# The chunk products of a bidirectional recurrence: the two heads of a pair, one after the other or in turns

## The chip, the cores and the metric

The kernel runs on one core of a Trainium2 chip. The metric is the device time of one execution in microseconds (us), taken as the median of several runs; lower is better.

## The reference, cut to what matters

One layer of a diffusion backbone: normalise and modulate the tokens, one input projection, then two mixers side by side (a bidirectional RWKV-7 recurrence with 8 heads of 64, and 4 heads of latent attention), an output projection, and a top-4-of-32 mixture of experts over 1024 tokens. The change touches the recurrence alone. Its definition, per direction `d`, head `h` and time step:

```python
def wkv_update(S, w_t, k_t, v_t, kk_t, a_t):
    """S: (2, B, H, N_v, N_k).  S <- S diag(w) + S (-kk)^T (kk*a) + v^T k."""
    sa = jnp.einsum("dbhvk,dbhk->dbhv", S, kk_t)
    return S * w_t[..., None, :] - sa[..., :, None] * (kk_t * a_t)[..., None, :] + v_t[..., :, None] * k_t[..., None, :]

def wkv_outputs(S0, r, ops):
    def step(S, inp):
        r_t, rest = inp
        S = wkv_update(S, *rest)
        return S, jnp.einsum("dbhvk,dbhk->dbhv", S, r_t)
    S, out = lax.scan(step, S0, (r, ops))
    return S, from_time_major(out)
```

First 256 context tokens are scanned for the state alone, then 1024 latent tokens for outputs.

## The kernel before, in words

**Chunks.** The recurrence is done in chunks of 64 tokens: 20 steps `j` of `Rwkv.scan` (line 2320), 4 of the context and 16 of the latent tokens, both directions at once. The 8 heads are 4 pairs (`q` or `hp`, 0 to 3); the two heads `h` of a pair lie on partitions 0 to 63 and 64 to 127 (`HS[0]`, `HS[1]`). Per step the operands of all pairs and both directions lie in a tile `W[:, d, q, 0:256]`: columns 0 to 63 for the outputs, 64 to 127 for the state, 128 to 255 the two keys.

**Products.** `Rwkv.products` (line 2143) makes, for each step, the matrix of in-chunk products `LM` that the scan multiplies by. For each pair, direction and head it is one fp32 matmul that contracts over the 64 partitions of the head, with 128 stationary columns (`x[:, 128:256]`) and 128 moving ones (`x[:, lo:128]`; 64 in a context step, where `lo` is 64). It goes over two halves `i` of the pairs and over `h`: four matmuls into one PSUM bank, then one VectorE multiply of the bank by the causal mask into `LM` (a "group"). A step has four groups, the kernel 80: 16 with 64 moving columns and 64 with 128. An fp32 matmul shows in the profile as two MATMUL records and two LDWEIGHTS records, so a group is 8 MATMUL records of the form 64\*128 64x128 (or 64x64). After the groups the same stream scales the keys on GpSimd (POOL), transposes them on TensorE into `BT`, and `states` (line 2171) copies columns; when all are done `ready[j]` is fired, which the scan waits for.

**What sets the order.** The whole stage is written as streams (Python generators) that are woven at build time by `Weave.run` (line 1033 on). A stream yields the name of an engine ("pe", "dve", "act", "pool", "sp") and then issues instructions there; `yield "pe", slots` asks for a turn of TensorE and a free bank out of `slots` at the same moment. The planner keeps a modelled time of every engine and of every buffer, takes the engine that can start soonest, and gives the turn to the ready stream of the smallest rank. The ranks: 0 for the scan and for the solver of the triangular systems, 30 for the work beside them, 49 to 81 for attention, 60 and 61 for readout and output mixing, 70 for the preparation of chunks with `products`, 100 for the chunk outputs. When its model of the TensorE clock is about to fall, attention (`dense`) goes first. The order of each engine's instructions is then fixed; at run time each engine goes through its own queue in that order and waits on semaphores. The modelled price of a product comes from `Timed.product` (line 915): the larger of the two column counts divided by 0.6 (0.3 at the lower clock), so 213 ns (427 ns) each, whatever stands beside it. The price isn't touched by the change. Every instruction woven in this way has line 954, that of the recording helper.

**Banks.** PSUM has eight banks. The scan has two of its own and the chunk outputs two more; the other four (`front.P`, here `self.B`) are shared by the products, the transposes, the solver, attention, readout and output mixing.

**Sets.** The operands of a step live in one of three sets (`self.SET`), so chunks are prepared at most three steps ahead of the scan.

After the mixers come output mixing, routing and the experts (`Experts`, lines 382 to 423 hold its matmuls and evictions), which run from about 1285 us to the end.

Of the kernel before, what the change touches and what calls it, by code (L numbers as in the profile page):

```python
# [30 lines left out]
HS = [slice(0, 64), slice(64, 128)]  # L31
# [148 lines left out]
class Experts:  # L180
# [190 lines left out]
    def products(self, J, s):  # L371
        nc, N = self.nc, J["N"]
        p = self.rings["pe"][0]
        self.rings["pe"].reverse()
        J["p", s] = p
        if s < 8:
            X = J["X"]
            xt = X.rearrange("p k s n -> p (k s n)").bitcast(BF).rearrange("p (k s n t) -> p k s n t", k=KT, s=2, t=2)
            wh, wl = (x.rearrange("p (k s c) -> p k s c", k=KT, s=2) for x in J.pop(("c", s)))
            for q in range(2):  # L380
                for k in range(KT):
                    nc.tensor.matmul(p[:, q, :2 * N], wh[:, k, q], X[:, k].rearrange("p s n -> p (s n)"),  # L382
                                     start=k == 0, stop=False, skip_group_check=True)
            for q in range(2):
                for k in range(KT):
                    nc.tensor.matmul(p[:, q, N:2 * N], wl[:, k, q], xt[:, k, 0, :, 1],  # L386
                                     start=False, stop=k == KT - 1, skip_group_check=True)
            return
        w = J.pop(("w", s)).rearrange("p (k s c) -> p k s c", k=KT, s=2)
        late = 1 if s == 8 else 0  # L390
        order = [(q, k) for q in range(2) for k in range(KT - late)] + [(q, k) for q in range(2) for k in range(KT - late, KT)]
        for q, k in order:
            nc.tensor.matmul(p[:, q, :N], w[:, k, q], J["H"][:, k], start=k == 0, stop=k == KT - 1, skip_group_check=True)  # L393
# [1656 lines left out]
class Rwkv:  # L2050
# [92 lines left out]
    def products(self, S, lo):  # L2143
        w, K, W, LM, j = self.w, self.K, S["W"], S["LM"], S["j"]
        msk = K("mask").rearrange("p (d o x) -> p d o x", o=1, d=2)[:, :, :, lo:].to_broadcast([128, 2, 2, 128 - lo])
        yield S["loaded"]
        left = [3]
        for i in range(2):
            for h in range(2):
                p = yield "pe", self.B  # L2150
                pv = p.rearrange("p (d q x) -> p d q x", d=2, q=2)
                for d in range(2):
                    for q in range(2):
                        x = W[HS[h], d, 2 * i + q]
                        w.pe.matmul(pv[:, d, q, lo:], x[:, 128:256], x[:, lo:128], start=True, stop=True)
                yield "dve"
                w.dve.tensor_mul(LM[:, :, 2 * i:2 * i + 2, h, lo:], pv[:, :, :, lo:], msk)
                w.put(self.B, p)
        w.spawn(70, self.states(S, left))
        for d in range(2):  # L2160
            yield "pool"
            w.pool.tensor_mul(W[:, d, :, 128:256], W[:, d, :, 128:256], S["lam"][:, d, :, None].to_broadcast([128, HP, 128]))
            p = yield "pe", self.B
            for hp in range(HP):
                w.pe.transpose(p[:, hp * 128:hp * 128 + 128], W[:, d, hp, 128:256], K("ident"))
            yield "act"
            w.act.activation(S["BT"][:, d].rearrange("p q x -> p (q x)"), p, AF.Copy)
            w.put(self.B, p)
            self.count(S, left)
# [742 lines left out]
```

## Time and profile before

| what | value |
|---|---|
| median of 3 runs | 2736.94 us (2735.51 to 2742.81) |
| the profiled execution | 2734.6 us, of which its span (first to last instruction) 2732.8 us |
| TensorE matmul busy (PE) | 2548.0 us, 93% |
| TensorE weight loads busy (PEld, beside PE) | 2240.4 us, 82% |
| VectorE (DVE) | 1889.3 us, 69% |
| ScalarE (ACT) | 1461.1 us, 53% |
| GpSimd (POOL) | 508.0 us, 19% |
| mean granted TensorE clock | 0.947 of full speed |

Busy times of different engines overlap. A matmul's record lasts until its result is written, so records of consecutive matmuls overlap too: what one more matmul costs is the distance between starts, not the record's length. The chain of waits is followed back from the last instruction: at each step to what released it, or else to the instruction before it on its engine.

### The profile page before, as it was taken

How to read it: one execution, taken by the hardware profiler on the slowest of the kernel's cores; microseconds unless marked ns; L12 is line 12 of the kernel's file. 1: busy time of each engine (PE TensorE's matmuls, PEld its weight loads, DVE VectorE, ACT ScalarE, POOL GpSimd, SP SyncE). 2: the span in 40 equal slices, each digit the busy share in tenths (PEclk: the TensorE clock that was granted, in tenths of full speed). 3: DMA queues.
4: the chain of work that ended last, by engine and by line, in shares of the span. 5: the costliest groups of instructions: out<-in, count | busy, mean ns of one | idle time of the engine just before them, and what ended most of it. 6: DMA issues, size and time to landing. Idle time of an engine off the chain costs nothing.

```text
span 2732.8 us, 58537 instructions
## 1 busy us (share of the span) xinstructions
PE 2548.0 (93%) x23428; PEld 2240.4 (82%) x23428; DVE 1889.3 (69%) x3925; ACT 1461.1 (53%) x2489; POOL 508.0 (19%) x455
## 2 busy tenths in 40 slices
PE   6999886989999997986999999999999999999996
PEld 3667664678677786665999999999999999999995
DVE  7745888867776638677676675766667676766765
ACT  6323333546544533234665665766656666666664
POOL 1112564411111136210011100110101010011101
PEclk8999987879999988997999999999999999999998
DMA  6741324253243145665887896988888988889884
GB/s 259 260 150 56 110 91 161 101 150 94 87 122 106 52 145 157 234 205 203 296 326 261 312 334 252 321 323 301 324 317 309 334 295 324 308 321 323 306 334 147
DMA packets 212183, 622.50 MB, mean 228 GB/s; under 512 B 49400, under 2 KB 127352, under 8 KB 160576
## 3 DMA queue, kind: packets, MB, share of 16 engines
q1 hardware_dynamic: 201008, 581.95, 59.1%
q0 software_dynamic: 10896, 36.74, 5.5%
q8 instruction: 186, 3.05, 0.4%
q14 instruction: 93, 0.76, 0.1%
HBM read 544.09 MB, written 74.53 MB: 226 GB/s over the span
## 4 chain that ended last, share of the span: by engine, by line
PE 72%; DVE 18%; DMA 3%; issue 3%; ACT 3%; POOL 1%; SPq 1%; DVEq 0%; ACTq 0%; POOLq 0%
PE banks L954 24%; PE banks L382 18%; PE banks L393 18%; DVE at L954 14%; PE banks L386 9%; ACT at L954 2%; DVE at L356 2%; PE banks L438 2%; PE banks L326 1%; POOL at L954 1%; DVE at L408 1%; SPq L954 1%; PE banks L292 0%; DVE at L409 0%; DMA at<-vh_d 0%
## 5 line engine op out<-in xcount | busy, mean ns | idle before, releaser
L954 PE MATMUL banks<-at,at 128*128 128x512 f32 (+10 forms) x3810 | 753.4, 355 | 54.4 <-POOL at L954 18.9
L954 PEld LDWEIGHTS banks<-at,at 128*128 128x128 f32 (+3 forms) x3290 | 451.4, 188 | 209.7 <-issue 82.3
L356 DVE TENSOR_TENSOR at<-at,at 128x2048 bf16<-128x2048 f32 x252 | 576.2, 2287 | 54.8 <-ACT at L348 53.9
L382 PE MATMUL banks<-at,at 128*128 128x256 f32 (+11 forms) x4096 | 601.8, 300 | 0.0
L382 PEld LDWEIGHTS banks<-at,at 128*128 128x128 f32 x4096 | 548.7, 190 | 1.2
L393 PE MATMUL banks<-at,at 128*128 128x128 f32 (+11 forms) x4096 | 521.5, 287 | 6.6 <-DVE at L417 6.0
L393 PEld LDWEIGHTS banks<-at,at 128*128 128x128 f32 x4096 | 505.0, 191 | 13.7 <-DVE at L417 12.9
L348 ACT ACTIVATE at<-at 128x2048 fp32r<-128x2048 f32 x252 | 481.5, 1911 | 0.0
L954 ACT ACTIVATE at<-banks 128x512 f32<-128x512 f32 (+6 forms) x475 | 239.6, 525 | 362.3 <-PE banks L954 339.5
L408 DVE TENSOR_TENSOR at<-banks,at 128x256 f32<-128x256 f32 (+11 forms) x256 | 115.6, 452 | 316.3 <-ACT at L407 304.3
L954 DVE TENSOR_TENSOR at<-at,at 128x1024 fp32r<-128x1024 f32 (+26 forms) x388 | 281.3, 736 | 57.0 <-ACT at L954 38.6
L407 ACT ACTIVATE at<-banks,at 128x128 f32<-128x128 f32 (+11 forms) x512 | 189.3, 380 | 226.1 <-PE banks L386 186.8
L386 PE MATMUL banks<-at,at 128*128 128x128 bf16 (+11 forms) x4096 | 306.0, 226 | 0.0
L954 ACT ACTIVATE at<-at 128x512 f32<-128x512 f32 (+10 forms) x259 | 175.9, 701 | 202.6 <-DVE at L954 108.3
L386 PEld LDWEIGHTS <-at 128*128 128x128 bf16 x4096 | 258.1, 96 | 17.6 <-issue 3.0
L954 PE MATMUL banks<-at 128*64 128x64 f32 (+4 forms) x4880 | 231.7, 232 | 36.8 <-DMA at<-w_d 18.6
L954 PEld LDWEIGHTS banks<-at 128*64 128x64 f32 (+3 forms) x4880 | 204.8, 143 | 68.7 <-issue 18.6
L954 POOL TENSOR_TENSOR at<-at,at 64x512 f32<-64x512 f32 (+5 forms) x130 | 185.9, 1439 | 308.0 <-DVE at L954 279.5
L423 ACT ACTIVATE at<-banks,at,modc 128x128 f32<-128x128 f32 (+11 forms) x256 | 116.9, 469 | 203.7 <-PE banks L393 203.5
L954 PE MATMUL banks<-kc,at 128*128 128x128 f32 (+4 forms) x1136 | 182.7, 291 | 44.5 <-ACT at L954 17.2
L312 POOL DMA_INDIRECT at<-h_d,at x49 | 47.5, 969 | 892.0 <-DVE at L294 364.1
L954 POOL TENSOR_TENSOR at<-at 128x512 f32<-128x512 f32 (+3 forms) x94 | 129.8, 1387 | 431.2 <-PE banks L954 132.3
(155 smaller groups left out, 2015.6 us busy)
## 6 DMA issues: line engine op xcount, KB each, us to landing
at<-in_wexp SPq DMA_DIRECT2D x384, 1024.0 KB
at<-in_mod_w SPq DMA_DIRECT2D x48, 512.0 KB
at<-w_d SPq DMA_DIRECT2D x48, 384.0 KB
w_d<-at SPq DMA_DIRECT2D x16, 1024.0 KB
at<-w_d SPq DMA_DIRECT2D x32, 512.0 KB
at<-in_w_in SPq DMA_DIRECT2D x18, 512.0 KB
x_d<-at SPq DMA_DIRECT2D x18, 512.0 KB
at<-in_x SPq DMA_DIRECT2D x16, 512.0 KB
```

The source lines that it names most:

```text
L312: nc.gpsimd.indirect_dma_start(out=xg[:R], out_offset=None, in_=self.d["h2"], in_offset=bass.IndirectOffsetOnAxis(ap=gi[:R, 0:1], axis=0))
L326: nc.tensor.transpose(p[:, k, :R], xg[:R, kk * 128:kk * 128 + 128], ident[:R, :R])
L348: self.nc.scalar.activation(wh, J["w", s], AF.Copy)
L356: self.nc.vector.tensor_sub(wl, J.pop(("w", s)), wh.bitcast(F32))
L382: nc.tensor.matmul(p[:, q, :2 * N], wh[:, k, q], X[:, k].rearrange("p s n -> p (s n)"), start=k == 0, stop=False, skip_group_check=True)
L386: nc.tensor.matmul(p[:, q, N:2 * N], wl[:, k, q], xt[:, k, 0, :, 1], start=False, stop=k == KT - 1, skip_group_check=True)
L393: nc.tensor.matmul(p[:, q, :N], w[:, k, q], J["H"][:, k], start=k == 0, stop=k == KT - 1, skip_group_check=True)
L407: nc.scalar.activation(u[:, q], p[:, q, N:2 * N], AF.Identity, bias=b)
L408: nc.vector.tensor_add(u, p[:, :, :N], u)
L423: nc.scalar.activation(J["yT"][:, c], p[:, q, :N], AF.Identity, bias=J["b2"][:, 8 + c:9 + c], scale=self.gt2[:, c:c + 1])
L438: nc.tensor.transpose(p[:R, k * 128:k * 128 + 128], J["yT"][:, 4 * j + k, b0:b0 + R], self.K("ident"))
L954: return f(*args, **kw)
```

## The change

The loop over `h` moves inside. A stream now asks for two turns of TensorE, each with a bank, and issues nothing in the first; in the second it issues the eight matmuls of a half of the pairs, with the two heads alternating, head 0 into the first bank and head 1 into the second. Then the two banks are masked one after the other, each in a VectorE turn of its own, and each is given back after its own mask. The number, shapes and operands of matmuls and masks stay as they are. Ranks, model prices and everything else in the kernel stay too; the planner weaves the whole stage anew.

```diff
         for i in range(2):
+            ps = [(yield "pe", self.B)]
+            ps.append((yield "pe", self.B))
+            views = [p.rearrange("p (d q x) -> p d q x", d=2, q=2) for p in ps]
+            for d in range(2):
+                for q in range(2):
+                    for h in range(2):
+                        x = W[HS[h], d, 2 * i + q]
+                        w.pe.matmul(views[h][:, d, q, lo:], x[:, 128:256], x[:, lo:128], start=True, stop=True)
             for h in range(2):
-                p = yield "pe", self.B
-                pv = p.rearrange("p (d q x) -> p d q x", d=2, q=2)
-                for d in range(2):
-                    for q in range(2):
-                        x = W[HS[h], d, 2 * i + q]
-                        w.pe.matmul(pv[:, d, q, lo:], x[:, 128:256], x[:, lo:128], start=True, stop=True)
                 yield "dve"
-                w.dve.tensor_mul(LM[:, :, 2 * i:2 * i + 2, h, lo:], pv[:, :, :, lo:], msk)
-                w.put(self.B, p)
+                w.dve.tensor_mul(LM[:, :, 2 * i:2 * i + 2, h, lo:], views[h][:, :, :, lo:], msk)
+                w.put(self.B, ps[h])
```

## Rows read from the trace of the kernel before

**Rows 1.** Busy time by engine in the stage of the recurrence, and in parts of it.
```profile
core 0: us, PE busy (x) PEld busy (x) DVE busy (x) ACT busy (x) POOL busy (x), PEclk, DMA share, GB/s
545.00:1130.00 585.00, 540.53 (x7020) 442.84 (x7021) 390.14 (x770) 267.43 (x494) 141.01 (x151) 0.90 0.39 118
...
950.00:1050.00 100.00, 92.05 (x1225) 81.16 (x1224) 50.04 (x92) 36.00 (x64) 38.84 (x43) 0.90 0.45 140
```

**Rows 2.** The chain of waits, 545 to 1130 us: shares; then pieces (start us, us, what).
```profile
by line: PE banks L954 54.3%; DVE at L954 28.9%; ACT at L954 4.6%; issue 4.1%; SPq L954 2.4%; DMA at<-vh_d 1.8%; POOL at L954 1.3%; DMA at<-v_d 0.7%; DMA at<-w_d 0.7%; DMA at<-in_w_out 0.6%; DMA at<-qr_d 0.4%; DMA at<-qn_d 0.4%; DVEq L954 0
...
954.88 28.98 PE banks L954 x283
```

**Rows 3.** Groups of instructions on PE, all of the span, shapes apart: the products.
```profile
L954 PE MATMUL banks<-at 64*128 64x128 f32 x512 | 75.6, 296 | 1.1 <-DVE at L954 1.1
...
L954 PE MATMUL banks<-at 64*128 64x64 f32 x128 | 19.3, 304 | 0.0
```

**Rows 4.** PE in order of time: one isolated group at full clock and what follows it.
```profile
start us, us, engine line op out<-in xcount [idle before <-releaser]
735.32 1.16 PE L954 MATMUL banks<-at 64*128 64x128 f32 x8
736.41 0.33 PE L954 MATMUL banks<-kc,at 128*128 128x128 f32 x1
```

**Rows 5.** PE in order of time, 954 to 970 us: groups at the lower clock.
```profile
954.88 1.34 PE L954 MATMUL banks<-at 64*128 64x128 f32 x8 [1.13 <-DVE at L954]
...
958.58 2.07 PE L954 MATMUL banks<-at 64*128 64x128 f32 x8
960.58 0.48 PE L954 MATMUL banks<-kc,at 128*128 128x128 f32 x1
...
963.12 2.07 PE L954 MATMUL banks<-at 64*128 64x128 f32 x8
965.12 2.50 PE L954 MATMUL banks<-at,at 128*128 128x128 f32 x10
967.55 2.07 PE L954 MATMUL banks<-at 64*128 64x128 f32 x8
```

**Rows 6.** PE in order of time: two groups that stand next to each other.
```profile
728.50 1.66 PE L954 MATMUL banks<-at 64*128 64x64 f32 x16
730.08 0.38 PE L954 MATMUL banks<-at,at 128*128 128x128 f32 x1
```

**Rows 7.** MATMUL records in flight in 10 ns: in Rows 4, in Rows 6, at lower clock.
```profile
core 0: us, PE busy (x), PEclk, DMA share, GB/s
735.90:735.91 0.01, 0.01 (x3) 1.00 0.00 0
729.33:729.34 0.01, 0.01 (x6) 1.00 0.00 0
...
964.00:964.01 0.01, 0.01 (x2) 0.50 1.11 410
```

**Rows 8.** Groups on DVE, 545 to 1130 us, shapes apart: the masks of latent steps first.
```profile
L954 DVE TENSOR_TENSOR at<-banks,kc 128x512 f32<-128x512 f32 x64 | 43.8, 689 | 34.5 <-PE banks L954 29.5 <-ACT at L954 4.2
...
L954 DVE TENSOR_TENSOR at<-banks,kc 128x256 f32<-128x256 f32 x50 | 19.4, 418 | 24.9 <-PE banks L954 14.0 <-ACT at L954 10.6
```

**Rows 9.** Who waited for whom on PE, 545 to 1130 us: us in total, times, longest.
```profile
engine line waited for: us in total, times, longest us
...
PE banks L954 <- DVE at L954: 25.9, 20, 4.8
...
PE banks L954 <- ACT at L954: 13.2, 10, 2.5
```

**Rows 10.** Groups on ACT, 545 to 1130 us: the evictions of full banks.
```profile
L954 ACT ACTIVATE at<-banks 128x512 f32<-128x512 f32 x181 | 105.3, 595 | 117.0 <-PE banks L954 112.7 <-DVE at L954 3.0
```

## The prediction

> **What bounds the kernel now.** The change sits in the stage from about 545 to 1130 us, so I read that stage and not the whole span. The busy times come first: TensorE works 540.5 of 585 us there, VectorE 390.1, ScalarE 267.4, GpSimd 141.0 [rows 1]. TensorE is 92% busy, also late in the stage when attention is over (92.05 of 100 us), and it stands still for 585 - 540.5 = 44.5 us. Its waits on VectorE and ScalarE make 25.9 and 13.2 us of that [rows 9]. The chain of waits says how much of the end hangs on it: 54.3% of the stage's chain lies on TensorE, 28.9% on VectorE, 4.6% on ScalarE [rows 2]. So a microsecond of TensorE work taken out of this stage brings about half a microsecond, and VectorE is what is late next. One piece of that chain shows the products on it: the 28.98 us from 954.88 us are TensorE alone [rows 2], and four groups of products begin inside them [rows 5].
>
> Then the products themselves. The form 64\*128 64x128 has 512 records and 64x64 has 128 [rows 3], so 80 groups of 8, or 40 pairs of groups. An isolated group at full clock, 8 records, begins at 735.32 and the next work at 736.41 [rows 4]: 1.09 us. At the lower clock (granted 0.50, the 1.2 GHz level) it takes 965.12 - 963.12 = 2.00 us [rows 5]. Counted through the whole stage in order of time, some 29 pairs consist of groups like the first, between 4 and 5 pairs run at the lower clock, and the groups of about 6 or 7 pairs stand right beside another group.
>
> Such neighbours are the evidence for this change. In rows 6 a context step's last group (head 1) is followed directly by a latent step's first group (head 0): other partitions, another bank. The 16 records take 730.08 - 728.50 = 1.58 us [rows 6] and not twice 1.09. Inside that stretch six MATMUL records are in flight at one moment, in the isolated group three [rows 7]. So the two halves of the array already work at the same time where the order happens to allow it.
>
> **The change part by part.**
>
> *Products of two heads in turns.* For two heads together the lower bound is one group's time, 1.09 us [rows 4], since every record then has a partner from the other half as in rows 7; the upper bound is 2.18 us, no gain. The neighbours at 1.58 us [rows 6] are between, because only the end of one group met the start of the next. I take 1.09 us, because six in flight against three is the full factor of two and alternating gives every matmul a partner from the start. Released on TensorE: 29 pairs at 2.18 - 1.09 = 1.09 us, 31.6 us; 4.5 pairs at the lower clock at 2.00 us, 9.0 us; 6.5 pairs that already overlap at 1.58 - 1.09 = 0.49 us, 3.2 us. Sum 44 us, between 0 and 44.
>
> *What reaches the end.* By the share of the chain, 0.543 of 44 us is 24 us [rows 2]. Not all of that lasts, since another chain closes in behind the shortened one: VectorE is 67% busy. I take a fifth off, 19 us; the ends are 0 and 44 us.
>
> *The masks move behind both heads.* Their number and size stay: a latent mask is 689 ns [rows 8]. Before, the mask of head 0 ran while TensorE went on; now two masks follow a pair, 1.38 us after 1.09 us of products. Where VectorE is the last to end (28.9% of the chain), the 0.29 us that TensorE no longer covers is paid: 40 x 0.29 x 0.289 = 3 us. It is 0 where other TensorE work stands between pairs, and 12 us if every pair pays. What is queued behind a mask on VectorE is the solver's multiplies and the scan's additions, both ahead of everything in rank, so a late mask delays them.
>
> *VectorE's wait in front of the masks.* VectorE idled 34.5 us ahead of latent masks, 29.5 us of it for TensorE [rows 8]. There is a reason in the code: the planner prices a group at 4 x 213 ns = 0.85 us, the chip takes 1.09 us, so masks were placed too early. After the change it prices eight matmuls at 1.70 us and the chip should take 1.09 us, so most of that idle time goes. Worth at most 29.5 x 0.289 = 8.5 us, at least nothing; I take half, 4 us.
>
> *Two turns and two banks.* No instruction is added. The stream takes a bank in its first turn, issues nothing, and holds the bank until a second turn with a second bank comes. By the waits on bank evictions that the stage has now (39.1 us on VectorE and ScalarE together [rows 9]) the shared four banks are not what TensorE waits for most, so I price this at nothing. What hides it is that other streams' products, transposes and scores still have two or three banks, each emptied in 595 ns [rows 10]. If that cover is gone, the second rival below has the price.
>
> *The order woven anew.* The planner's turns shift, so the whole stage gets another order. No row shows that order. Nearest are the single waits of TensorE for VectorE and ScalarE: 30 of them, 39.1 us, 1.3 us each [rows 9]. Five more or five fewer are 6 us either way; I take zero.
>
> Sum: -19 + 3 - 4 = -20 us. Against the profiled execution's own 2734.6 us that is 2714.6 us; that execution lies 2.3 us under the median of the runs, 2736.94 us, so the forecast is 2717 us.
>
> The masks are also where a rule speaks against the change. The rows show VectorE waiting in front of the masks, not TensorE waiting for them [rows 8]. The Trainium skill, TensorEngine Tiling (Array Packing), section Performance Considerations, warns that tiling speeds up TensorE but not the emptying of PSUM, which may become the bottleneck. By that rule every pair would cost its two masks' 1.38 us; 32 us would be released and not 44, 14 us of it would reach the end, the 3 us for the masks would fall away as counted already, and the forecast would be about 2719 us; by the rows it is 2717 us.
>
> **The rivals.**
>
> *All of the released time counts.* For: the 29 us piece of pure TensorE in the chain [rows 2], and a stage in which TensorE is 92% busy throughout [rows 1]. Against: 28.9% of the chain is VectorE's. It would give 2736.9 - 44 = 2693 us.
>
> *Nothing that reaches the end.* The released time turns into more standstill on TensorE, because the scan's own chain (its additions, the solver, loads and sets) sets the pace, or the heads don't overlap as hoped because the weight loads of both halves queue. For: VectorE's and the loads' share of the chain. Against: TensorE's share, and rows 6 and 7, where weights were loaded for both halves too. It gives 2733 to 2737 us.
>
> *The banks run short, slower.* Its place: between a pair's two turns, when one of the four shared banks lies empty and reserved and two more wait for their masks. If TensorE then stands still until a ScalarE eviction (595 ns [rows 10]) and a mask (689 ns [rows 8]) are over, a pair pays 1.28 us, 40 pairs 51 us, against 44 us released: some 7 to 8 us slower where all of it is on the path, 2745 us. The point from which it decides is 44 / 40 = 1.1 us of standstill per pair. For: attention, readout, solver and mixing all draw on those four banks. Against: TensorE's 39.1 us of such waits in the whole stage [rows 9].
>
> **How the numbers follow.** A measurement of this kernel can tell about 0.3% (8 us) from no change. Chances: the forecast 0.55, all of it counts 0.16, nothing reaches the end 0.17, banks run short 0.12. Faster by over 0.3% is then 0.71, within 0.3% 0.17, slower 0.12. The likeliest case alone spans 2707 to 2730 us: with 12 us instead of 3 for the masks and nothing for the wait it is 2730, with no fifth taken off and 8.5 us for the wait 2707. The range reaches down to the case in which everything counts and up to the last case's beginning: 2692 to 2744 us. Outside are the worse half of the last case and large shifts of the order, together less than 2 in 10.
>
> **What would show it.** Right: in order of time the products stand as 40 blocks of 16 records, each about 1.1 us to the next work at full clock, with about six records in flight; TensorE's busy time in the stage falls by about 40 us while the stage itself ends about 20 us earlier; VectorE's idle time before the masks shrinks. The experts after it take as long as before. Wrong: blocks of 16 that take about 2 us (no overlap); TensorE's waits on VectorE and ScalarE well above 39 us (banks); or a stage as long as before with more standstill on TensorE (hidden).

## The result, and the profile after

The changed kernel takes 2772.81 us (median of 4 runs, 2767.42 to 2781.11) against 2736.35 us of the kernel before (4 runs): ratio 1.0131, 95% interval 1.0101 to 1.0160. The forecast was 2717 us, faster. It is 36 us slower, outside the range, and on the other side.

Busy time by engine in the stage of the recurrence, kernel after; it answers to [rows 1].

```profile
core 0: us, PE busy (x) PEld busy (x) DVE busy (x) ACT busy (x) POOL busy (x), PEclk, DMA share, GB/s
545.00:1130.00 585.00, 495.11 (x6990) 401.42 (x6990) 370.94 (x741) 264.29 (x483) 136.57 (x153) 0.89 0.39 118
```

TensorE's busy time fell from 540.5 to 495.1 us, as the change meant it to. But the window is the same length, so TensorE now stands still for 90 of 585 us where it stood still for 44.5 us. The time was released and turned into waiting.

The products themselves, groups on PE with shapes apart, kernel after; they answer to [rows 3].

```profile
L954 PE MATMUL banks<-at 64*128 64x128 f32 x512 | 42.3, 300 | 2.1 <-DVE at L954 1.7 <-ACT at L954 0.5
...
L954 PE MATMUL banks<-at 64*128 64x64 f32 x128 | 12.0, 316 | 2.5 <-DVE at L954 2.4
```

75.6 + 19.3 us have become 42.3 + 12.0 us: 40.6 us less. One block in order of time, kernel after, at full clock; it answers to [rows 4].

```profile
778.71 1.16 PE L954 MATMUL banks<-at 64*128 64x128 f32 x16
779.80 0.44 PE L954 MATMUL banks<-kc,at 128*128 128x128 f32 x2
```

Both heads, 16 records, take 779.80 - 778.71 = 1.09 us, exactly what one head took before. At the lower clock it is the same: a block and the wait before it, order of time, kernel after; it answers to [rows 5].

```profile
812.76 0.82 PE L954 MATMUL banks<-kc,at 128*128 128x128 f32 x5 [2.91 <-DVE at L954]
813.51 2.08 PE L954 MATMUL banks<-at 64*128 64x128 f32 x16
815.52 0.69 PE L954 MATMUL banks<-kc,at 128*128 128x128 f32 x2
```

2.01 us for both heads, with a clock granted at 0.50. Records in flight in 10 ns, kernel after; the rows answer to [rows 7].

```profile
core 0: us, PE busy (x), PEclk, DMA share, GB/s
772.60:772.61 0.01, 0.01 (x6) 1.00 0.57 205
814.20:814.21 0.01, 0.01 (x4) 0.50 0.00 0
```

Six in flight at full clock and four at the lower one, where an isolated group had three and two. All 640 records stand in 40 blocks of 16. The alternation works. What went wrong shows in who waited for whom on PE, 545 to 1130 us, kernel after; it answers to [rows 9].

```profile
engine line waited for: us in total, times, longest us
...
PE banks L954 <- DVE at L954: 51.7, 35, 11.3
PE banks L954 <- ACT at L954: 22.8, 25, 2.5
```

TensorE waited 74.5 us for VectorE and ScalarE, before 39.1 us. (The row of 812.76 above is one of these waits, 2.91 us.) The first matmuls of the experts began at 1306.5 us, before at 1267.9 us (somewhat ahead of the 1285 us at which the experts were said to begin): the first and last starts of line 382, kernel after and then kernel before.

```profile
L382 PEld LDWEIGHTS banks<-at,at x4096: 186/188/338, 1306.5 to 2720.1; 128*128 128x128 f32 x196
```

```profile
L382 PEld LDWEIGHTS banks<-at,at x4096: 186/188/338, 1267.9 to 2681.3; 128*128 128x128 f32 x196
```

The experts take 1413.6 us from first to last in one and 1413.4 us in the other. So practically all of the 39 us between the two profiled executions arises before them. Part of it is seen in attention: in the kernel before its last score product on 64 rows starts at 946 us, in the changed kernel ten records of such products (two to a product) still run after 947 us, the last from 997 us on.

```profile
L954 PE MATMUL banks<-at,at 64*128 64x512 f32 x6 | 3.3, 545 | 0.0
...
L954 PE MATMUL banks<-at,at 64*128 64x256 f32 x4 | 1.7, 430 | 0.0
```

(Groups on PE, 947 to 1130 us, kernel after; the kernel before has none.) The masks of latent steps, groups on DVE, 545 to 1130 us, kernel after, answer to [rows 8]:

```profile
L954 DVE TENSOR_TENSOR at<-banks,kc 128x512 f32<-128x512 f32 x64 | 44.0, 688 | 25.4 <-PE banks L954 23.0
```

### The profile page after: what moved, and what is told of

The parts are those of the page before. It is cut to its first block, busy times and chain, and to the rows that moved or that the text cites. A ratio compares the mean times of both kernels' runs of the same rounds, so it can differ in the third digit from the quotient of the medians.

```text
span 2771.8 us, 58552 instructions
## 1 busy us (share of the span) xinstructions
PE 2527.6 (91%) x23428; PEld 2213.8 (80%) x23428; DVE 1896.9 (68%) x3925; ACT 1469.6 (53%) x2489; POOL 497.6 (18%) x455
## 4 chain that ended last, share of the span: by engine, by line
PE 68%; DVE 18%; issue 4%; DMA 4%; ACT 3%; POOL 1%; SPq 1%; DVEq 0%; ACTq 0%; POOLq 0%
PE banks L954 21%; PE banks L382 18%; PE banks L393 17%; DVE at L954 14%; PE banks L386 9%; ACT at L954 2%; DVE at L356 2%; PE banks L438 2%; PE banks L326 1%; POOL at L954 1%; DMA at<-w_d 1%; DVE at L408 1%; SPq L954 1%; DMA at<-y_d 1%; DMA at<-in_x 0%
## 5 line engine op out<-in xcount | busy, mean ns | idle before, releaser
L954 PE MATMUL banks<-at,at 128*128 128x512 f32 (+9 forms) x3810 | 765.3, 359 | 86.3 <-ACT at L954 40.2
L954 PEld LDWEIGHTS banks<-at,at 128*128 128x128 f32 (+3 forms) x3290 | 457.1, 191 | 245.2 <-issue 82.3
L393 PEld LDWEIGHTS banks<-at,at 128*128 128x128 f32 x4096 | 505.0, 191 | 14.0 <-DVE at L417 13.2
L954 DVE TENSOR_TENSOR at<-at,at 128x512 f32<-128x512 f32 (+26 forms) x388 | 281.9, 738 | 58.2 <-ACT at L954 39.2
L954 POOL TENSOR_TENSOR at<-at,at 64x512 f32<-64x512 f32 (+6 forms) x130 | 188.6, 1459 | 304.2 <-DVE at L954 281.2
L954 PE MATMUL banks<-at 128*64 128x64 f32 (+4 forms) x4880 | 193.4, 233 | 49.7 <-DVE at L954 31.8
L954 PEld LDWEIGHTS banks<-at 128*64 128x64 f32 (+3 forms) x4880 | 169.4, 143 | 76.6 <-DVE at L954 31.7
L954 PEld LDWEIGHTS banks<-kc,at 128*128 128x128 f32 (+2 forms) x1136 | 143.8, 172 | 88.6 <-issue 34.6
```

The costliest lines, as they stand in the source:

```text
L954: return f(*args, **kw)
```

## The experiments

Three explanations were on the table: the alternation itself costs something; the second bank, above all while it is reserved and empty, starves the other streams; the planner weaves worse, because it counts a block at 1.70 us that takes 1.09 us, or simply because a new weave is a new draw, another order of the same work that may be good or bad by chance. Ratios are to the kernel before, run on the same chip beside each experiment; it came out between 2734 and 2740 us there.

**e1, alternation undone, order kept.** The planner's price doesn't depend on the order inside a turn, so this kernel and the changed one have the same order everywhere else; in the two traces the 3925 instructions of VectorE, 2489 of ScalarE and 455 of GpSimd indeed follow in the same sequence of forms.

```diff
-            for d in range(2):
-                for q in range(2):
-                    for h in range(2):
+            for h in range(2):
+                for d in range(2):
+                    for q in range(2):
```

> The changed kernel with one thing undone: in the two-bank turn the four products of head 0 are issued first and the four of head 1 after them. The planner's prices are the same, so the order of every engine is that of the changed kernel. Theory A (alternating does what was forecast, the loss of 36 us comes from the new order and the banks): slower than the changed kernel, whose blocks take 1.09 us, by 40 blocks x (1.58 - 1.09) us = 20 us times the chain's share of TensorE there (0.37): 7 to 15 us, so 2780 to 2788 us. Rival (alternating itself costs something, because matmuls on both halves hinder neighbours or each other): as fast as or faster than the changed kernel, 2772 us or less.

Measured: 2772.12 us, ratio 1.0116 (1.0061 to 1.0172): the changed kernel's 2772.81 us. A block, order of time, kernel e1:

```profile
774.62 1.71 PE L954 MATMUL banks<-at 64*128 64x128 f32 x16
776.26 0.44 PE L954 MATMUL banks<-kc,at 128*128 128x128 f32 x2
```

Blocks take 1.64 us in place of 1.09 us, and nothing of it is seen at the end. Where it went stands in the busy times and in the waits of PE, 545 to 1130 us, kernel e1:

```profile
545.00:1130.00 585.00, 512.27 (x6975) 420.95 (x6976) 367.23 (x735) 259.16 (x474) 133.59 (x152) 0.89 0.39 116
```

```profile
PE banks L954 <- DVE at L954: 40.9, 26, 10.8
PE banks L954 <- ACT at L954: 18.4, 20, 2.5
```

TensorE is busy 17.2 us longer than in the changed kernel, and waits 59.3 us for VectorE and ScalarE where that waits 74.5 us: 15.2 us less. So in this order what the blocks save is spent waiting. Theory A's 2780 to 2788 us failed. The time is where the rival put it, but not for the rival's reason: alternating makes the blocks shorter, so it hinders nothing. With four runs on each side, a gain of up to some 7 us could not be told from none.

**e2, the two banks in one turn.** A small class stands for "two free banks", so nothing is reserved empty.

```diff
-            ps = [(yield "pe", self.B)]
-            ps.append((yield "pe", self.B))
+            ps = yield "pe", Two(self.B)
```

> The changed kernel, but the two banks are asked for in one turn, so none is reserved and empty while the second is awaited. Bank theory (the reserved empty bank starves the other streams): most of the loss returns, 2725 to 2750 us. Price theory (the planner counts 1.70 us for a block that takes 1.09 us, and weaves the rest around it): as slow as the changed kernel, 2760 to 2785 us.

Measured: 2754.98 us, ratio 1.0073 (1.0045 to 1.0101): about half of the loss returns, between the ranges of both theories.

**e3, the price that the trace shows.** In the planner's `product`:

```diff
+            elif (k, m) == (64, 128) and n in (64, 128):
+                ns = 136 if fast else 250
             else:
                 ns = big / (0.6 if fast else 0.3)
```

> The changed kernel, but the planner prices a product at 136 ns (250 ns at the lower clock), the 1.09 us that a block of eight took in the trace, in place of 213 ns (427 ns). Price theory: most of the loss returns, 2715 to 2745 us. Bank theory: the reserved bank is still there, 2755 to 2780 us.

Measured: 2750.23 us, ratio 1.0047 (1.0022 to 1.0072). Also more than half, but not the 2745 us that the price alone was to reach.

**e4, a fifth shared bank.**

```diff
-        self.CH, self.PO, self.B = Slots(chain[0:2]), Slots(chain[2:4]), banks
+        self.CH, self.PO, self.B, self.more = Slots(chain[0:1]), Slots(chain[2:4]), banks, chain[1]
...
         yield begin
+        w.put(self.B, self.more)
...
-        for s in (r.CH, r.CH, r.PO, r.PO):
+        for s in (r.CH, r.PO, r.PO):
```

> The changed kernel with a fifth shared bank, taken from the scan, which keeps one of its two (its three uses follow one another). Bank theory: the cost of the second bank is paid for, 2715 to 2745 us. Price theory: little changes, 2760 to 2785 us. If any new weave moves the time by tens of us whatever is changed, the time may land anywhere between 2720 and 2790 us, and e2 to e4 will not line up with either theory.

Measured: 2745.66 us, ratio 1.0031 (1.0003 to 1.0058), just above the bank theory's range and far below the price theory's. Three different remedies each return about half or more. Either each theory is half right, or every new weave is a new draw and 2773 us was a bad one. That was the next question.

**e5 to e7, new draws without any change in what is issued.** The same two lines as in e3, with prices a hair off the old ones.

```diff
+            elif (k, m) == (64, 128) and n in (64, 128):
+                ns = 209 if fast else 418
```

> The kernel before with one number of its planner changed: a product is priced at 209 ns in place of 213 ns (418 ns in place of 427 ns at the lower clock). No product is issued in another way; only the weave is drawn anew. Theory W (the kernel before holds an order that any new weave loses, whatever is changed): 2750 to 2775 us. Theory T (the turn with two banks is itself what costs): within 0.4% of before, 2725 to 2747 us.

> A second such draw: the kernel before with a product priced at 215 ns (430 ns). Theory W: 2740 to 2770 us, and not the same as the draw at 209 ns. Theory T: 2725 to 2747 us.

> The changed kernel with the same change of one number, 209 ns in place of 213 ns. Theory W: another draw of the same lottery, anywhere from 2740 to 2785 us, and overlapping the draws of the kernel before. Theory T: the turn with two banks is still there, 2762 to 2785 us.

Measured: the kernel before 2755.70 us at 209 ns (ratio 1.0056, 1.0029 to 1.0083) and 2748.32 us at 215 ns (1.0039, 1.0018 to 1.0060); the changed kernel 2741.17 us at 209 ns (1.0010, 0.9986 to 1.0034). A price changed by 2% costs the kernel before 16 us and gives the changed kernel 32 us. All three times lie in theory W's ranges and outside theory T's. So the order of the kernel before looks like a good draw, and that of the changed one like a bad draw; the table further down has five draws of each.

**e8, both remedies together** (the edits of e3 and e4).

> The changed kernel with both remedies: a block at the price that the trace shows (136 ns a product, 250 ns at the lower clock) and a fifth shared bank from the scan. If banks and price are two separate costs, their gains (27 us for the bank, 23 us for the price) add up: about 2722 us, faster than before. If both remedies were only new draws of the weave: between 2735 and 2775 us.

Measured: 2708.07 us, ratio 0.9881 (0.9847 to 0.9915), faster than both kernels, and 14 us below even the sum of the two gains. Busy times and the start of the experts, kernel e8:

```profile
545.00:1130.00 585.00, 523.72 (x7256) 424.82 (x7256) 413.67 (x854) 276.24 (x521) 147.91 (x162) 0.93 0.45 139
```

```profile
L382 PEld LDWEIGHTS banks<-at,at x4096: 186/188/338, 1240.8 to 2653.4; 128*128 128x128 f32 x196
```

More instructions fit in the same 585 us (7256 on PE against 6990), and the experts start 66 us earlier than in the changed kernel, 27 us earlier than before.

**e9, the alternation in a good order** (the edit of e1 on e8).

> The kernel of e8 (true price, fifth bank), with the four products of head 0 issued before the four of head 1, as e1 did to the changed kernel. The order of all else is that of e8. Theory: where TensorE is kept full, the alternation pays what it releases: blocks grow from 1.09 to 1.64 us, 40 x 0.55 = 22 us, of which a third to a half reaches the end, so 7 to 14 us slower than e8, 2715 to 2722 us. Rival: as in e1 nothing reaches the end, and e8 owes its time to the weave alone: 2704 to 2712 us.

Measured: 2717.49 us (2712.63 to 2720.24), ratio 0.9933 (0.9910 to 0.9955). Head after head is 9 us slower than e8 (2705.64 to 2712.73 us), with every other instruction in the same order, as the theory had it and not the rival. The 9 us are rough, some 4 to 13 us by the spread of the runs: the two ran on different chips, and the intervals of their ratios touch. Nothing seen of 22 us in e1 and 9 us here: as far as these runs tell, the same edit is worth what the surrounding order lets through. More than half of what e8 gains on the kernel before stays without the alternation.

**e10, the reserved bank alone, on the kernel before.**

```diff
+                z = yield "pe", self.B
                 p = yield "pe", self.B
...
                 w.put(self.B, p)
+                w.put(self.B, z)
```

> The kernel before, with its four turns and its order of products, but each group first reserves a bank that it never uses, in a turn of its own, and gives it back with its own. That is the suspected cost of the changed kernel alone and twice over (80 reservations in place of 40), without any alternation. Bank theory: 2770 to 2810 us, above all five draws seen so far of either form (2739 to 2773 us). If the reserved bank is harmless: within those draws, 2735 to 2770 us.

Measured: 2786.46 us, ratio 1.0189 (1.0149 to 1.0230): slower than any draw of either form. Busy times and waits on PE, 545 to 1130 us, kernel e10:

```profile
545.00:1130.00 585.00, 522.83 (x6670) 428.75 (x6669) 362.71 (x729) 254.95 (x466) 124.03 (x138) 0.90 0.39 117
```

```profile
PE banks L954 <- DVE at L954: 38.8, 28, 8.2
PE banks L954 <- ACT at L954: 18.1, 21, 2.8
```

350 fewer PE instructions got done in the window than in the kernel before [rows 1], and the waits for VectorE and ScalarE grew from 25.9 and 13.2 us [rows 9] to 38.8 and 18.1 us. It is a single draw of its kind, and it holds the unused bank until the mask is done, longer than the changed kernel's reservation lasts; but it lies 14 us beyond the worst of the ten draws of both forms in the table below, and 29 us beyond the worst of its own form.

**e11, the fifth bank on the kernel before** (the edit of e4).

> The kernel before with the fifth shared bank alone. If the four banks hold that kernel back too: 2715 to 2732 us, below its draws (2739, 2756, 2748 us). If the fifth bank only pays for the second bank of a turn: another draw, 2735 to 2765 us.

Measured: 2755.24 us, ratio 1.0069 (1.0041 to 1.0097). Another draw; a fifth bank by itself does nothing that can be told from the lottery.

**e12 to e16, more draws, in pairs at the same price.**

> The changed kernel with a product priced at 215 ns (430 ns), the pair of e6. The lottery alone: anywhere from 2735 to 2775 us. If the turn with two banks costs something beside the lottery: above e6's 2748 us, 2755 to 2780 us.

> The kernel before with a product priced at 217 ns (434 ns). Lottery: anywhere from 2738 to 2765 us, and its own 2739 us is at the good end of its draws.

> The changed kernel with a product priced at 217 ns (434 ns). If the form costs some 10 us beside the lottery: 2745 to 2780 us, and the mean of its draws stays 5 to 15 us above that of the kernel before. If the form costs nothing: the means come together within 5 us.

> The kernel before with a product priced at 220 ns (440 ns). As e13: 2738 to 2765 us.

> The changed kernel with a product priced at 220 ns (440 ns). As e14: 2745 to 2780 us if the form costs some 10 us, 2738 to 2765 us if it costs nothing.

| price of a product | form before, us (ratio) | changed form, us (ratio) | difference of the ratios | TensorE's waits, form before, us | TensorE's waits, changed form, us |
|---|---|---|---|---|---|
| 209 ns | 2755.70 (1.0056) | 2741.17 (1.0010) | -0.46% | 51.9 | 78.9 |
| 213 ns | 2736.35 (1) | 2772.81 (1.0131) | +1.31% | 39.1 | 74.5 |
| 215 ns | 2748.32 (1.0039) | 2759.78 (1.0083) | +0.44% | 42.7 | 66.3 |
| 217 ns | 2745.52 (1.0032) | 2756.01 (1.0072) | +0.40% | 50.3 | 81.6 |
| 220 ns | 2757.71 (1.0090) | 2758.76 (1.0080) | -0.10% | 46.2 | 74.7 |
| mean | 1.0043 | 1.0075 | +0.32% | 46.0 | 75.2 |

e12, e13, e15 and e16 lie in the ranges named for the lottery; e12, e14 and e16 also lie in those named for a cost of the form. The differences have a spread of 0.67%, so their mean of 0.32%, 9 us, has a 95% interval of about -0.5% to +1.2% (five pairs). That the changed form costs anything by itself, at the planner's old price and with four banks, isn't settled. That it doesn't bring the forecast 20 us (0.73%) is: the interval leaves that out, and no pair reaches it.

The last two columns are TensorE's waits for VectorE and ScalarE together, 545 to 1130 us of each profiled execution. They hold what the draws of a form have in common. The rows of the changed form's best draw, kernel e7 (its recording helper has line 956):

```profile
PE banks L956 <- DVE at L956: 43.0, 31, 6.2
PE banks L956 <- ACT at L956: 35.9, 25, 8.4
```

Each draw of the changed form, good or bad, waits longer than each draw of the form before, by 29 us in the mean; and TensorE is busy 32 us less in the same window (487 to 504 us against 522 to 541 us). So the released time became waiting in every order that was drawn, and the waits are not what made 2773 us a bad draw. The granted clock of the whole execution differs as well: in the median of the runs 0.936 to 0.942 in the changed form's draws, 0.943 to 0.947 in the others. Runs of the kernel before alone reach from 2719.99 us at 0.951 to 2752.68 us at 0.939 (beside e13), so a difference of 0.005 goes along with some 10 to 15 us, an estimate from these runs; whether the clock is a cause of the 9 us or a consequence of the waits isn't shown.

**e17, e18, is e8 more than a draw?** Two further draws of e8.

> The kernel of e8 with a product priced at 134 ns (246 ns) in place of 136 ns (250 ns). If the remedies make the gain: below every draw of either form so far (2739 to 2773 us), 2700 to 2730 us. If e8 was one good draw: 2735 to 2765 us.

> The kernel of e8 with a product priced at 138 ns (254 ns). As e17: 2700 to 2730 us if the remedies make the gain, 2735 to 2765 us if it was one good draw.

Measured: 2747.09 us (ratio 1.0032, 1.0006 to 1.0059) and 2725.02 us (0.9949, 0.9928 to 0.9969). The three lie 39 us apart. e17 lands in the range for one good draw, e18 in that for the remedies. Their mean ratio is 0.9954, below the means of both forms (1.0043 and 1.0075), and two of the three are below all ten of those draws. TensorE's waits for VectorE and ScalarE are 45.8, 56.5 and 53.2 us in e8, e17 and e18, close to those of the form before. With three draws the mean is below that of the changed form by 1.2%, give or take 1.0%, and below that of the form before by 0.9%, give or take 0.9% (95%, if the groups spread alike): that the remedies help the changed form is likely, that the result beats the form before isn't settled, and how much of e8's 2708 us is a good draw three draws can't tell. The form before with its own true price (1.09 us for four products) and a fifth bank was not run, so it is open whether this gain needs the changed form at all.

## Why the prediction was wrong, point by point

**The products: right.** 1.09 us for both heads at full clock, 2.01 us at the lower one, six records in flight, forty blocks. Released were 40.6 us by the groups' busy time, against a forecast of 44 us. The evidence in [rows 6, 7] was enough for this.

**What reaches the end: the first step that failed.** The prediction took 54.3% of the released time by TensorE's share in the chain, less a fifth, 19 us. In place of that, TensorE's waits for VectorE and ScalarE took the released time up: 29 us more of them in the mean of five pairs, and a mean of +9 us (-14 to +31) where -20 us was forecast. So this step failed whatever order was drawn. The share belongs to the order of the kernel before; in the changed kernel's order it is 37.3%. In that order e1 shows 0 of 22 us, in e8's order e9 shows 9 of 22 us, which is about what 54.3% less a fifth would give. The share of a chain is a price for one order. Of the 35 us by which the waits grew in the first pair, 15 hang on the alternation (e1 against the changed kernel); what the two turns, the two banks and the later masks add to the rest isn't separated, and no run tests the 3 us for the masks behind both heads by themselves.

**The order woven anew: the step that turned a miss into a loss of 36 us.** It was priced at zero, plus or minus 6 us, worked out from single waits of 1.3 us. The draws measure it: from 2736 to 2758 us in the form before, from 2741 to 2773 us in the changed one, with nothing else changed than a price by a few per cent. By the table's means, the 36 us are made of 12 us by which the kernel before is better than its own draws, 15 us by which the changed kernel is worse than its own, and 9 us between the forms, which may be nothing. So of the 56 us between forecast and result, by these means, 27 us are the luck of two draws and 29 us are not (each give or take some 20 us). Single waits are no bound for a new order: in e5, where nothing but a price changed, 739 of the 3925 places in VectorE's sequence hold another form of instruction than in the kernel before.

**Two turns and two banks: priced at nothing, open.** The waits of TensorE on VectorE and ScalarE were named as the sign, "well above 39 us (banks)", and they are 74.5 us; the other sign of being wrong, more standstill on TensorE, came too, so the signs don't tell the last two rivals apart. The rival of the banks (the third; the prediction calls it the second where it prices the banks) had the right side but 2745 us for a price, and that TensorE stands still between a pair's two turns isn't shown. e10, a single draw, points to a cost of reserving banks in this stage. e2 and e4 ease the banks and are faster than the changed kernel, but by amounts within the lottery; what the reservation costs in the changed kernel isn't known.

**VectorE's wait in front of the masks: right in direction, small.** It was to lose most of 29.5 us and went to 23.0 us. The reason given, a price of 0.85 us for a group of 1.09 us and then 1.70 us for a block of 1.09 us, points at the planner's price: with it corrected and a fifth bank given, the three draws average 33 us below those of the changed form (0.9954 against 1.0075). Which of the two does it, single draws of each (e3, e4) don't tell.

**The rule weighed against the change.** The Trainium skill, TensorEngine Tiling (Array Packing), section Performance Considerations, warns that emptying PSUM may become the bottleneck after a fourfold speedup of TensorE; the products here became twice as fast. No run here isolates it. The masks still wait for TensorE (23.0 us, [rows 8 and their answer above]), which speaks against it; that TensorE's waits for VectorE and ScalarE grew in all five pairs speaks for it, though e1, with slower blocks of 1.64 us, has 59.3 of the 74.5 us too.

## What to carry to other kernels

Where a planner or list scheduler weaves a stage, a change of one stream redraws the order of all of them: before a difference of 1% is given to an edit, draw both forms several times with a neutral change (a price off by 1 or 2%) and compare the groups. What all draws of a form share, here 29 us more waiting, belongs to the edit; what differs between them belongs to the draw. Test the edit itself in a fixed order, as e1 and e9 did, and correct the planner's price together with the code, since it goes on scheduling around a cost that is gone (what that alone is worth these runs don't settle). The products here, fp32 over 64 partitions, cost half when the two halves of the array take turns into two banks, but that paid only where the order that resulted let it through: about 9 us in e9, nothing seen in e1.

## What was not expected of the hardware

Two groups in succession overlap without being interleaved. In e1 four products of one head follow four of the other, and the 16 records take 1.64 us and not twice 1.09 us; the pair of [rows 6] in the kernel before, with a context group first, takes 1.58 us. In the block of e1 shown above the second head's first record starts 0.55 us after the first head's, when three of the first head's eight are still to start: 0.55 + 1.09 = 1.64 us. Turns one by one take 1.09 us, so a plain sequence on the two halves already has half of the gain, 0.54 of 1.09 us.
